# A third key group of the first memory taken from the opening of a two-block transformer kernel and put into the last norm of its first part

## The chip, the cores and the metric

The kernel runs on one core of a Trainium2 chip. The metric is the device time of one execution in microseconds (us); a lower time is better. Three runs of the kernel before gave 1830.6, 1832.58 and 1834.89 us, median 1832.58.

The core has a matrix engine (TensorE, PE in the profile, with PEld for its weight loads), a vector engine (VectorE, DVE), an activation engine (ScalarE, ACT), GpSimd (POOL), and SyncE (SP), which in this kernel only issues DMAs. Each engine works through its own list of instructions in the order in which the list was written, and waits where an operand is not there yet.

## The reference

Two blocks of two layers each work on 256 tokens of 1024 values in float32. What matters here is how the first block begins, how it ends, and what the second block takes from a memory of another 256 tokens (`mem`):

```python
def first_block(x, c, ...):
    c_act = jax.nn.silu(c)
    for l in range(DEPTH):                                     # DEPTH = 2
        mod = c_act @ w_ada[l] + b_ada[l]                      # 6 x 1024 values
        sh1, sc1, g1, sh2, sc2, g2 = [t[:, None, :] for t in jnp.split(mod, N_ADA, axis=-1)]
        h = rmsnorm(x, norm_mix_g[l]) * (1.0 + sc1) + sh1
        z = h @ w_in[l]
        o = jnp.concatenate([swa_mixer(...), mla_mixer(...), nsa_mixer(...), moba_mixer(...)], axis=-1)
        x = x + g1 * (o @ w_out[l])
        h = rmsnorm(x, norm_mlp_g[l]) * (1.0 + sc2) + sh2
        x = x + g2 * (jnp.square(jax.nn.relu(h @ w_up[l])) @ w_down[l])
    return rmsnorm(x, final_norm_g)                            # the "last norm"

def second_block(x, mem, ...):
    for layer in range(DEPTH):
        proj = jnp.einsum('bsd,de->bse', x, w_in[layer])       # z, xbc, dt_raw, ...
        ...
        mem_kv = jnp.einsum('bmd,de->bme', mem, w_mem_kv[layer]).reshape(
            Bsz, MEM_TOKENS, 2, CROSS_HEADS, CROSS_HEAD_DIM)
        oc = _memory_cross_attention(cq, mem_kv)
        ...
```

The keys and values of the memory (`mem_kv`) do not depend on `x`. So the kernel is free to compute those of the second block's first layer, "the first memory", whenever TensorE has nothing else to do.

## The kernel before

**Numbers.** Each float32 matrix is split into a high half and a low half, and each product is made of three matmuls: high by high, low by high, high by low. For a weight, a tile `w` of 128 x 1024 (512 KB, one DMA from SP, L289), the high half `wh` is a cast on ACT (L299) and the low half `wl` a subtraction on DVE (L301). There are 8 buffers for raw weights (`NW`) and 4 for each half (`NS`). `next_w` hands out the next weight and issues loads and splits for those behind it in one long list (`e.wq`, filled by `stream`), so the order of that list is the order of the weights. The weights `w_ada` are used raw by TensorE, and are never split.

**The first memory.** `mem_gemm` makes one of six groups. Groups 0 to 3 are keys (`w_mk` in the profile): two weights, 48 matmuls of 128 x 256 into a bank `g`, and a copy of that bank on ACT into `mk` (L488). Groups 4 and 5 are values (`w_mv`): four weights, 48 matmuls of 128 x 512 into two banks, and two copies into `mv` (L490). Group 4 is called v0 below, group 5 v1, and the key groups k0 to k3.

**The opening.** TensorE runs k0, k1, k2, k3 and v0, and between them the eight pieces `a0` of the first two rows (shift and scale) of `mod`: each piece is two raw weights, 16 small matmuls (`ada`, 128 x 32 by 128 x 256). Which pieces go with which group stands in the table `start`. After four pieces `ada_end` copies the row to `pt1` (ACT, L567), transposes it with matmuls `adat`, and adds the bias on DVE (`mod`, L572). Once the entries tagged `start2` have been issued, the statistics of the first norm are issued: four squares on ACT (L451), which share the two buffers of `pt1` with the row copy; folds on DVE (L438, L444); a matmul `st` that sums over the partitions; `rv` on DVE (L420), `rsy` on POOL (L403), and `bc`, the matmuls that spread the result. `norm_apply` then makes `nt` (DVE, L603), `ah` (ACT, L604) and `al` (DVE, L605), which the first projection's matmuls `g<-ah,wh` and `g<-al,wh` read.

**The last norm of the first block** (L1084 to 1098): `acc`, the accumulators of the last MLP, are added to `x` (L1085); then comes v1, written ahead of `norm_stats(x)`; then the same chain of squares, folds, `st`, `rv`, `rsy`, `bc`; then `x` times `bc` (L1095), split into `xh` (ACT, L464) and `xl` (DVE, L465), which the second block's first matmuls `dt` and `g` read.

**What sets the order.** A scheduler places each instruction by the program's order and by two offsets of priority: splits of weights (`SPLIT_FIRST`, 100) and norms with `ada_end` (`NORM_FIRST`, 200) may move ahead of what was written before them. On DVE the last norm's loop (L1093 to 1097) is kept in its written order.

Of the kernel before, what the change touches and what calls it, by code (L numbers as in the profile page):

```python
# [480 lines left out]
MEM_KEYS = lambda l: [("w2_mk", l, g) for g in range(4)] + [("w2_mv", l, g) for g in range(2)]  # L481


def mem_gemm(e, l, i, hl, mk, mv, tag="mem"):

    key = MEM_KEYS(l)[i]
    if i < 4:
        e.gemm(tag, [key], lambda _: hl, lambda ps: e.nc.scalar.copy(mk[:, 2 * i : 2 * i + 2, :], v3(ps, 2)))  # L488
    else:
        e.tok_gemm(tag, key, hl, lambda ps, t: e.nc.scalar.copy(mv[:, t, (i - 4) * 512 : (i - 3) * 512], ps))  # L490
# [3 lines left out]
def block1(e, ctx, mem0):  # L494
# [3 lines left out]
    mhl, mk0, mv0 = mem0  # L498
# [11 lines left out]
    ad_mlp = lambda l: [(1,0),(1,1)] if l == 0 else [(1,5)]  # L510
    ad_next = lambda l: ada(l+1,2)+ada(l+1,3)
    mlp_keys = lambda l: {1 + 6 * i + n: [("w_ada", *p, n)] for i, p in enumerate(ad_mlp(l)) for n in range(4)}
    MEM = 5
    a0 = ada(0, 0) + ada(0, 1)
    start = [[], a0[0:2], a0[2:4], a0[4:6], []]
    for k in range(MEM):
        e.stream(MEM_KEYS(0)[k], *start[k])
    half = e.wq[-2:]
    del e.wq[-2:]
    e.stream(*a0[6:8])  # L520
# [1 line left out]
    for l in range(DEPTH):  # L522
# [9 lines left out]
                e.stream(("w_down", l, g - 1))  # L532
            e.stream(*nxt.get(g, []))
        e.stream(("w_down", l, 15), *([("w_in1", l + 1, zorder[0])] if l + 1 < DEPTH else []), *ad_next(l))
    e.stream(*MEM_KEYS(0)[MEM:])


    th = e.t(cp, [P, KC], "cth")
# [53 lines left out]
    def ada_add(tag, keys):  # L592
        for key in keys:
            e.add(tag, lambda key=key: (ada_pool if tag == "mlp" else ada_step)(*key[1:]))
# [10 lines left out]
                nc.vector.scalar_tensor_tensor(al[:, k, :], tt, sh[:, k : k + 1], ah[:, k, :].bitcast(F32), ALU.add, ALU.subtract)  # L605


    for g in range(MEM):
        mem_gemm(e, 0, g, mhl, mk0, mv0, f"start{g}")
        ada_add(f"start{g}", start[g])  # L610
    half = e.q[-2:]
    del e.q[-2:]
    ada_add("start4", a0[6:8])
# [470 lines left out]
        for k in range(KC):  # L1084
            nc.vector.scalar_tensor_tensor(x[:, k, :], acc[k // 2][:, (k % 2) * S : (k % 2 + 1) * S], mod[:, 40 + k : 41 + k], x[:, k, :], ALU.mult, ALU.add)  # L1085

    for k in range(MEM, 6):
        mem_gemm(e, 0, k, box[0], mk0, mv0)
    bc = norm_stats(x)
    e.need("mem")  # L1090
# [607 lines left out]
def emit(tc, d, out):  # L1698
    with ExitStack() as ctx:
        e = Emit(tc, d, ctx)  # L1700
        mhl = load_mem(e)
        mk, mv = v3(e.unit("mk"), KC), v3(e.unit("mv"), 2)
        with ExitStack() as inner:
            xh, xl = block1(e, inner, (mhl, mk, mv))
        with ExitStack() as inner:
            block2(e, inner, xh, xl, mk, mv, out)
# [21 lines left out]
```

## Time and profile before

| | before |
|---|---|
| median of 3 runs | 1832.58 us (1830.6 to 1834.89) |
| the profiled execution | 1832.16 us |
| its span (first to last instruction) | 1830.3 us |
| mean granted TensorE clock | 0.991 |
| PE / DVE / ACT busy | 1789.1 / 1333.6 / 1016.8 us |

The profiled execution lies 0.42 us below the median, and its span 1.9 us below its own time. Of the two stretches that the change touches, the opening reaches from 0 to about 62 us, and the last norm from about 744 to 764 us. PE counts as busy as long as its matmuls run, also where they run at the lower of TensorE's two clocks; "PEclk" is the granted share, 1.00 for 2.4 GHz and 0.50 for 1.2 GHz.

### The profile page before, as it was taken

How to read it: one execution, taken by the hardware profiler on the slowest of the kernel's cores; microseconds unless marked ns; L12 is line 12 of the kernel's file. 1: busy time of each engine (PE TensorE's matmuls, PEld its weight loads, DVE VectorE, ACT ScalarE, POOL GpSimd, SP SyncE). 2: the span in 40 equal slices, each digit the busy share in tenths (PEclk: the TensorE clock that was granted, in tenths of full speed). 3: DMA queues.
4: the chain of work that ended last, by engine and by line, in shares of the span. 5: the costliest groups of instructions: out<-in, count | busy, mean ns of one | idle time of the engine just before them, and what ended most of it. 6: DMA issues, size and time to landing. Idle time of an engine off the chain costs nothing.

```text
span 1830.3 us, 36255 instructions
## 1 busy us (share of the span) xinstructions
PE 1789.1 (98%) x14344; PEld 1674.3 (91%) x14344; DVE 1333.6 (73%) x2209; ACT 1016.8 (56%) x1882; POOL 359.1 (20%) x291
## 2 busy tenths in 40 slices
PE   7999999999998999999999999999999999999998
PEld 6778799987888999998999999999999999999997
DVE  4575775756778655798897997576788797997566
ACT  4444444434555444567777575454556777675552
POOL 0000281800007200002444202200001444202200
PEclk9999999999998999999999999999999999999999
DMA  9873876758348655553444644465554445544451
GB/s 335 308 249 138 310 259 199 256 197 306 115 140 299 226 183 185 165 175 121 162 162 151 202 155 144 168 208 173 194 176 133 148 160 162 184 164 165 154 181 67
DMA packets 98219, 346.82 MB, mean 189 GB/s; under 512 B 12288, under 2 KB 13440, under 8 KB 97792
## 3 DMA queue, kind: packets, MB, share of 16 engines
q1 hardware_dynamic: 98048, 344.50, 55.5%
q8 instruction: 112, 1.84, 0.4%
q14 instruction: 59, 0.48, 0.1%
HBM read 339.01 MB, written 1.05 MB: 186 GB/s over the span
## 4 chain that ended last, share of the span: by engine, by line
PE 89%; DVE 4%; DMA 3%; ACT 3%; issue 1%; SPq 0%; POOLq 0%; DVEq 0%; POOL 0%; ACTq 0%
PE g L337 67%; PE acc L337 10%; PE yps L337 2%; DVE wl L301 1%; ACT wh L299 1%; PE ada L337 1%; PE o L337 1%; PE ds L337 1%; PE sc L337 1%; DMA w<-w_in 1%; PE do L337 1%; DMA w<-w_ada 1%; ACT sb L683 1%; PE xo L337 1%; DMA w<-w_up 1%
## 5 line engine op out<-in xcount | busy, mean ns | idle before, releaser
L301 DVE TENSOR_TENSOR wl<-w,wh 128x1024 fp32r<-128x1024 f32 x518 | 660.8, 1279 | 342.8 <-ACT wh L299 341.1
L299 ACT CAST wh<-w 128x1024 fp32r<-128x1024 f32 x518 | 540.5, 1047 | 494.9 <-PE g L337 328.8
L337 PE MATMUL g<-xh,wh 128*128 128x256 f32 x1664 | 478.2, 288 | 0.3
L337 PE MATMUL g<-xl,wh 128*128 128x256 f32 x1664 | 472.6, 284 | 0.0
L337 PE MATMUL g<-xh,wl 128*128 128x256 f32 x1664 | 471.8, 284 | 0.0
L337 PEld LDWEIGHTS g<-xh,wh 128*128 128x128 f32 x1664 | 319.8, 192 | 12.6 <-issue 6.2
L337 PEld LDWEIGHTS g<-xl,wh 128*128 128x128 f32 x1664 | 319.8, 192 | 0.9 <-issue 0.7
L337 PEld LDWEIGHTS g<-xh,wl 128*128 128x128 f32 x1664 | 319.9, 192 | 0.0
L337 PE MATMUL g<-ah,wh 128*128 128x256 f32 x736 | 211.5, 289 | 5.9 <-ACT ah L604 5.4
L337 PE MATMUL g<-ah,wl 128*128 128x256 f32 x736 | 210.6, 287 | 0.5 <-DVE wl L301 0.5
L337 PE MATMUL g<-al,wh 128*128 128x256 f32 x736 | 210.5, 287 | 0.5 <-DVE al L605 0.5
L403 POOL TENSOR_TENSOR rsy<-rv,mhalf 128x2 f32<-128x2 f32 (+1 forms) x14 | 14.5, 1038 | 936.8 <-DVE rv L420 830.1
L337 PE MATMUL acc<-pt,wh 128*128 128x256 f32 x1024 | 182.9, 280 | 0.0
L1505 POOL PARTITION_BROADCAST E<-rows x64 | 98.0, 1592 | 386.7 <-PE tw L1209 190.9
L1504 ACT ACTIVATE E<-E,ltok 128x128 f32<-128x128 f32 x384 | 124.3, 394 | 60.2 <-POOL E L1505 56.8
L337 PEld LDWEIGHTS acc<-pt,wh 128*128 128x128 f32 x1024 | 156.8, 188 | 0.5 <-issue 0.4
L337 PEld LDWEIGHTS g<-ah,wh 128*128 128x128 f32 x736 | 142.7, 195 | 9.8 <-ACT ah L604 6.4
L337 PEld LDWEIGHTS g<-al,wh 128*128 128x128 f32 x736 | 142.8, 194 | 2.7 <-DVE al L605 1.4
L337 PEld LDWEIGHTS g<-ah,wl 128*128 128x128 f32 x736 | 142.8, 194 | 1.2 <-DVE wl L301 0.7
L337 PE MATMUL acc<-pt,wl 128*128 128x256 f32 x512 | 142.3, 279 | 0.0
L583 POOL TENSOR_SCALAR sb<-w,ca 128x1024 f32<-128x1024 f32 x24 | 90.0, 3751 | 59.9 <-PE ada L337 32.8
L337 PEld LDWEIGHTS acc<-pt,wl 128*128 128x128 f32 x512 | 96.2, 188 | 0.0
(384 smaller groups left out, 3404.8 us busy)
## 6 DMA issues: line engine op xcount, KB each, us to landing
w<-w_ada SPq DMA_DIRECT2D x96, 512.0 KB
w<-w_up SPq DMA_DIRECT2D x64, 512.0 KB
w<-w_down SPq DMA_DIRECT2D x64, 512.0 KB
w<-w_br SPq DMA_DIRECT2D x64, 512.0 KB
w<-w_gl SPq DMA_DIRECT2D x48, 512.0 KB
w<-w_in SPq DMA_DIRECT2D x36, 512.0 KB
w<-w_xs SPq DMA_DIRECT2D x32, 512.0 KB
w<-w_z SPq DMA_DIRECT2D x32, 512.0 KB
```

Of the source, the lines that this page charges most:

```text
L299: nc.scalar.copy(wh, w)
L301: nc.vector.tensor_tensor(wl, w, wh.bitcast(F32), ALU.subtract)
L337: self.last_mm = self.nc.tensor.matmul(o, l, r, start=start, stop=stop)
L403: self.nc.gpsimd.tensor_tensor(y, v, self.mhalf[:, 0:cols], ALU.pow)
L583: nc.gpsimd.tensor_scalar(dst, w, ca[:, 2 * n + i : 2 * n + i + 1], None, ALU.mult)
L683: nc.scalar.activation(self.src(i), self.src(i), AF.Exp, bias=nmx[:, i : i + 1], scale=scale, accum_out=den[:, i : i + 1])
L1504: ex = lambda o, s, r: nc.scalar.activation(o, o, AF.Exp, bias=bias[:, s, r : r + 1])
L1505: nc.gpsimd.partition_broadcast(E, state["rows"][32 * (h % 4) : 32 * (h % 4) + 1, :])
```

## The change

The six groups are divided into `early` (k0, k1, k2, v0), which stay in the opening, and `late` (k3, v1), which are made in the last norm, k3 first. The pieces of `a0` that stood behind k3 now stand with those behind k2, so four pieces follow k2 in a row. The tag `start2`, which is waited for ahead of `x`'s statistics, now covers all four of them.

```diff
-    MEM = 5
+    early, late = (0, 1, 2, 4), (3, 5)
     a0 = ada(0, 0) + ada(0, 1)
-    start = [[], a0[0:2], a0[2:4], a0[4:6], []]
-    for k in range(MEM):
-        e.stream(MEM_KEYS(0)[k], *start[k])
+    start = [[], a0[0:2], a0[2:6], []]
+    for i, k in enumerate(early):
+        e.stream(MEM_KEYS(0)[k], *start[i])
     half = e.wq[-2:]
     del e.wq[-2:]
     e.stream(*a0[6:8])
...
-    e.stream(*MEM_KEYS(0)[MEM:])
+    e.stream(*(MEM_KEYS(0)[k] for k in late))
...
-    for g in range(MEM):
-        mem_gemm(e, 0, g, mhl, mk0, mv0, f"start{g}")
-        ada_add(f"start{g}", start[g])
+    for i, k in enumerate(early):
+        mem_gemm(e, 0, k, mhl, mk0, mv0, f"start{i}")
+        ada_add(f"start{i}", start[i])
...
-    for k in range(MEM, 6):
+    for k in late:
         mem_gemm(e, 0, k, box[0], mk0, mv0)
     bc = norm_stats(x)
```

The number of instructions on each engine stays the same; only their order changes.

On TensorE in the opening, before, right behind the two `ada` pieces that follow k2 (`ada_265`) comes k3 (`g_411`), with `adat` inside it, then two more pieces (`ada_469`), `st`, and v0 (`g_500`, `g_507`):

```order
152 L337 MATMUL ada_265<-w_208,ca_11_101 32x256 x4
153 L337 MATMUL g_411<-mh_77,wh_236 128x256
...
176 L337 MATMUL adat_382<-pack_1_70,pt_64_380 128x4 x2
...
203 L337 MATMUL ada_469<-w_276,ca_11_101 32x256 x3
...
206 L337 MATMUL ada_469<-w_295,ca_11_101 32x256 x4
207 L337 MATMUL st_401<-ones_72,fold_392 128x1 x2
208 L337 MATMUL g_500<-wh_323,mh_77 128x512
209 L337 MATMUL g_507<-wh_323,mh_77 128x512
210 L337 MATMUL g_500<-wl_325,mh_77 128x512
```

After, at the same place (`ada_259` is the first row of `mod`, `ada_374` the second, `g_438` and `g_445` are v0):

```order
152 L337 MATMUL ada_259<-w_208,ca_11_101 32x256 x4
153 L337 MATMUL ada_374<-w_264,ca_11_101 32x256 x4
154 L337 MATMUL ada_374<-w_270,ca_11_101 32x256 x4
155 L337 MATMUL adat_370<-pack_1_70,pt_58_368 128x4 x2
156 L337 MATMUL ada_374<-w_276,ca_11_101 32x256 x4
157 L337 MATMUL ada_374<-w_283,ca_11_101 32x256 x4
158 L337 MATMUL g_438<-wh_287,mh_77 128x512
159 L337 MATMUL g_445<-wh_287,mh_77 128x512
160 L337 MATMUL st_426<-ones_72,fold_417 128x1 x2
161 L337 MATMUL g_438<-wl_289,mh_77 128x512
```

The 48 matmuls of k3 are gone from between the row's pieces, and `st` now stands behind the first two matmuls of v0.

On ACT at the same place, after: the copy of k2's bank, the row copy, the four squares, and only then the casts for v0 (`wh_287`, `wh_293`):

```order
12 L488 COPY mk_85<-g_282 128x512
13 L567 COPY pt_58_368<-ada_259 128x256
14 L451 ACTIVATE pt_72_413<-x_411 128x512
15 L451 ACTIVATE pt_73_415<-x_411 128x512
16 L451 ACTIVATE pt_75_419<-x_411 128x512
17 L451 ACTIVATE pt_76_422<-x_411 128x512
18 L299 CAST wh_287<-w_285 128x1024
19 L299 CAST wh_293<-w_291 128x1024
```

Before, two casts for k3 stood between the bank's copy and the row copy, and the copy of k3's bank between the squares and v0's casts.

On DVE in the last norm, before, the four subtractions for the second block's first weights (`wl_8488` to `wl_8506`) all stand ahead of the first two `x` (L1095):

```order
781 L444 TENSOR_TENSOR fold_8355<-fold_8355 128x256
782 L301 TENSOR_TENSOR wl_8500<-w_8496,wh_8498 128x1024
783 L420 TENSOR_SCALAR rv_8367<-st_8364 128x2
784 L301 TENSOR_TENSOR wl_8506<-w_8502,wh_8504 128x1024
785 L1095 SCALAR_TENSOR_TENSOR x_386<-x_386,pack_1_70,bc_8371 128x256 x2
786 L465 TENSOR_TENSOR xl_8431<-x_386,xh_8430 128x256
```

After, at the same place:

```order
778 L444 TENSOR_TENSOR fold_8297<-fold_8297 128x256
779 L301 TENSOR_TENSOR wl_8488<-w_8484,wh_8486 128x1024
780 L301 TENSOR_TENSOR wl_8494<-w_8490,wh_8492 128x1024
781 L420 TENSOR_SCALAR rv_8309<-st_8306 128x2
782 L301 TENSOR_TENSOR wl_8500<-w_8496,wh_8498 128x1024
783 L1095 SCALAR_TENSOR_TENSOR x_411<-x_411,pack_1_70,bc_8313 128x256 x2
784 L301 TENSOR_TENSOR wl_8506<-w_8502,wh_8504 128x1024
785 L465 TENSOR_TENSOR xl_8431<-x_411,xh_8430 128x256
```

The last of the four subtractions now stands between the first two `x` and the first `xl`. On TensorE k3's bank `g_8316` stands between `acc` and v1, and `st` 12 matmuls of v1's last weight and 3 more ahead of `bc`.

## Rows read from the trace of the kernel before

**Rows 1.** The page: busy time of the engines, and the chain of waits by engine
```profile
PE 1789.1 (98%) x14344; PEld 1674.3 (91%) x14344; DVE 1333.6 (73%) x2209; ACT 1016.8 (56%) x1882; POOL 359.1 (20%) x291
...
PE 89%; DVE 4%; DMA 3%; ACT 3%; issue 1%; SPq 0%; POOLq 0%; DVEq 0%; POOL 0%; ACTq 0%
```

**Rows 2.** Windows: length, busy PE, PEld, DVE, ACT, POOL; PEclk, DMA share, GB/s
```profile
40.00:45.00 5.00, 5.00 (x57) 3.93 (x56) 2.84 (x5) 3.52 (x5) 0.00 (x0) 1.00 0.79 296
...
58.00:64.00 6.00, 3.97 (x22) 2.93 (x22) 4.76 (x9) 3.64 (x7) 0.00 (x0) 1.00 1.00 379
...
214.00:221.00 7.00, 6.05 (x26) 5.75 (x27) 6.44 (x15) 3.38 (x8) 3.04 (x2) 0.51 1.02 413
...
528.00:534.00 6.00, 4.55 (x33) 3.63 (x34) 4.85 (x14) 4.34 (x11) 0.00 (x0) 1.00 0.11 33
...
756.00:764.00 8.00, 6.88 (x34) 6.69 (x35) 6.79 (x17) 3.24 (x9) 0.00 (x0) 0.57 0.37 116
764.00:768.00 4.00, 4.00 (x36) 4.00 (x35) 0.03 (x1) 1.10 (x2) 0.00 (x0) 1.00 0.00 0
```

**Rows 3.** The chain of waits: start, length, what
```profile
26.82 5.96 PE g L337 x48
...
743.99 10.47 PE g L337 x46
```

**Rows 4.** PE's timeline, opening: start, length, what [idle before, what ended it]
```profile
32.70 1.93 PE L337 MATMUL ada<-w,ca 128*32 128x256 f32 x32
...
45.47 0.50 PE L337 MATMUL g<-wl,mh 128*128 128x512 f32 x1
...
53.36 0.72 PE L337 MATMUL g<-wh,mh 128*128 128x512 f32 x2
...
61.16 0.38 PE L337 MATMUL g<-ah,wh 128*128 128x256 f32 x1 [1.54 <-ACT ah L604]
```

**Rows 5.** SP's timeline, opening: DMA issues
```profile
25.58 0.80 SPq L289 DMA_DIRECT2D w<-w_mk  x2
26.45 7.75 SPq L289 DMA_DIRECT2D w<-w_ada  x4
```

**Rows 6.** ACT's timeline, opening
```profile
38.86 0.63 ACT L451 ACTIVATE pt<-x 128x512 f32<-128x512 f32 x1 [2.78 <-PE adat L337]
40.25 1.15 ACT L451 ACTIVATE pt<-x 128x512 f32<-128x512 f32 x2 [0.76 <-DVE fold L438]
```

**Rows 7.** DVE's timeline, opening
```profile
42.44 0.43 DVE L444 TENSOR_TENSOR fold<-fold 128x256 f32<-128x256 f32 x1
44.19 1.23 DVE L301 TENSOR_TENSOR wl<-w,wh 128x1024 fp32r<-128x1024 f32 x1 [1.33 <-ACT wh L299]
```

**Rows 8.** PE's timeline, other places where PE waited
```profile
214.43 0.79 PE L337 MATMUL g<-ah,wh 128*128 128x256 f32 x2 [2.31 <-ACT ah L604]
...
529.42 1.44 PE L708 MATMUL tp<-pack,sb 128*128 128x128 f32 x6 [1.80 <-DVE sb L695]
```

**Rows 9.** PE's timeline, last norm
```profile
755.84 0.71 PE L337 MATMUL bc<-pack,rsy 128*128 128x128 f32 x4 [1.05 <-POOL rsy L403]
757.67 0.58 PE L337 MATMUL dt<-xh,wh 128*128 128x256 f32 x1 [1.12 <-ACT xh L464]
...
758.48 0.41 PE L337 MATMUL dt<-xl,wh 128*128 128x256 f32 x1
758.69 0.41 PE L337 MATMUL dt<-xh,wl 128*128 128x256 f32 x1
```

**Rows 10.** DVE's timeline, last norm
```profile
755.56 1.23 DVE L301 TENSOR_TENSOR wl<-w,wh 128x1024 fp32r<-128x1024 f32 x1 [0.58 <-ACT wh L299]
756.71 0.87 DVE L1095 SCALAR_TENSOR_TENSOR x<-x,pack,bc 128x256 f32<-128x256 f32 x2
757.65 0.42 DVE L465 TENSOR_TENSOR xl<-x,xh 128x256 fp32r<-128x256 f32 x1
```

## The prediction, made before the changed kernel had run

> **What bounds the kernel now.** I read the page's busy times first, then its chain: PE is busy for 1789.1 us of the 1830.3 us span and holds 89% of the chain [rows 1]. So what counts is how many matmuls PE has to run, at which clock, and how long it waits. The change leaves the number of matmuls as it is. It can only move time between the two stretches that it touches, so I read the windows of these two next, then the timelines of PE, ACT and DVE in them. The windows show that around the opening's end the DMA engines are at their limit (share 1.00 at 58 to 64 us), but that PE is busy while k3 runs, for 5.00 of 5.00 us at 40 to 45 us, and at full clock [rows 2]. The last norm runs at a low clock, 0.57 from 756 to 764 us, and is back at 1.00 from 764 us [rows 2].
>
> **What goes from the opening.** A key group is 48 matmuls in 5.96 us, 0.124 us each [rows 3]. If nothing replaced it, the opening would be 5.96 us shorter. But k3 was also what PE worked on while the statistics of `x` were made. The two `ada` pieces behind k2 begin at 32.70 and take 1.93 us [rows 4]; up to 34.6 us nothing changes. Now the next two pieces (1.86 us) and `adat` (0.34 us) follow at once, so PE reaches v0 at 34.6 + 2.2 = 36.8 us. Their weights are there: in the list of loads they take the places of k3's two and of the first two behind these, issued at 25.58 us and from 26.45 us on [rows 5], when buffers came free that the change leaves alone.
>
> What isn't there is the first half of v0. Its cast stands behind the four squares on ACT. The second square waits for `adat`, since row copy and squares share two buffers; it began at 38.86 us before [rows 6]. Now `adat` stands behind two of the four weights, at 34.6 + 0.93 = 35.5 us, so the second square can begin at 36.1 us, 2.76 us earlier. From that square on nothing shortens the chain: squares three and four begin 1.39 us later (40.25 - 38.86) and take 1.15 us together [rows 6], so ACT is free at 36.1 + 1.39 + 1.15 - 0.1 = 38.55 us, the first cast takes 1.05 us, and the first v0 matmuls can run at 39.65 us. The folds end at 42.44 + 0.43 = 42.87 us before [rows 7], so at 40.1 us now, and behind them DVE makes the first subtraction, 1.23 us [rows 7]: 41.35 us. PE's third v0 matmul, the first that reads it, begins at 41.4 us, against 45.47 us before [rows 4]. That is 4.1 us. From there on PE's list is as before up to the end of the row's pieces, but for the `st` that has moved ahead (0.3 us): v0's second half, begun at 53.36 us before [rows 4], begins at 48.95 us. I take 4.4 us. So 1.5 to 2 us of the key group's time turn into waiting, 36.8 to 39.65 and, after two matmuls and `st`, 40.3 to 41.4 us: 3.9 us in all.
>
> The first norm's end stays tied to that: `adat` of the second row now stands behind all 24 matmuls of v0's second half, not behind 12 of them, but a subtraction that stood between `A` and `nt` is gone. These two are within 0.5 us of each other, so I cost them at nothing together.
>
> **The clock there.** PE has waits with and without a drop of the clock behind them. A wait of 2.31 us at 214 us is followed by 7 us at 0.51, but one of 1.80 us at 529 us and one of 1.54 us at 61 us are not followed by any [rows 2, 4, 8]. The new wait of 2.85 us, with 1.1 us more close behind, is longer than the longest of these three, so I expect a drop. What a drop costs is read in the last norm: from 758.48 us the 128 x 256 matmuls follow each other at 0.21 us [rows 9], against 0.124 us at full clock, until about 763.8 us. That is 25 matmuls in 5.3 us which would take 3.1 us, so a drop costs 2.2 to 2.3 us. Bounds for this term: 0 (no drop) and 3 us, if the seven microseconds of the spell at 214 us were all spent on matmuls at 0.21 us (33 of them, 0.086 us lost on each). I take 2.3, the row nearest in kind. The opening then gains 4.4 - 2.3 = 2.1 us.
>
> **What comes to the last norm.** Before, v1 holds PE from 743.99 us on for 10.47 us with 46 of its matmuls, 0.2276 us each [rows 3]; two stand earlier, among the last `acc`. Now two matmuls of k3 stand there, 0.2 us shorter, so `acc` ends at 743.8 us. Then come 46 of k3 (46 x 0.12 = 5.5 us; its halves are split ahead, beside `acc`), 48 of v1 (10.9 us) and `st` (0.35 us): `bc` could begin at 760.5 us. It began at 755.84 us, after a wait of 1.05 us for `rsy` [rows 9]. That wait goes, because `st` now stands 15 matmuls (3.4 us) ahead of the end, and `rv` and `rsy` lie beside these. So `bc` comes 4.7 us later: 5.75 us for a key group, less 1.05 us.
>
> Behind `bc` a new link stands on DVE: `bc` to `x` 0.8 us, two `x` 0.87 us, then the subtraction that had been done before the first `x` begins (755.56 us, 1.23 us) [rows 10], then the first `xl`, 0.42 us. The subtraction waits for a cast, which waits for v1's last matmul because it takes that weight's buffer; the cast ends 1.05 us behind it, at 761.5 us, beside `bc` and `x`, and is not the limit. The first `xl` matmul comes 0.8 + 0.87 + 1.15 + 0.42 = 3.2 us behind `bc`'s start, where before it came 758.48 - 755.84 = 2.64 us behind it [rows 9]. On PE `dt` and two `g` wait for `xh` in between, as before. So the second block's matmuls begin 4.7 + 0.6 = 5.2 us later (rounded down, since the 0.2 us at `acc` may be more).
>
> The clock there: before, PE waited 1.05 and 1.12 us around `bc` and the clock fell [rows 2, 9]. Now only the waits behind `bc` are left, 1.3 and 0.5 us. If it falls all the same, the shift is 5.2 us; if not, 5.2 - 2.3 = 2.9 us. I hold the first for likelier (0.6), since the idle time from the last v1 matmul to the first `xl` matmul is much the same.
>
> **The rest.** The order moves by a few rows in the mixers of both layers and ahead of the second block; loads run ahead of PE there, so I take 0, with 1 us on either side.
>
> **The sum.** -4.4 + 2.3 + 5.2 = +3.1 us against the profiled execution's 1832.16 us: 1835.2 us. The median of the runs shown is 0.4 us higher, which is inside the rounding.
>
> **The rivals.**
> (a) Both stretches gain: PE's waits in the opening are too short to lower the clock, and the shorter waits in the last norm leave it high. Then 1832.2 - 4.4 + 2.9 = 1830.7 us; with the key group's whole 5.96 us, if v0's cast were done in the squares' waits, 1829.1 us. For it speaks that the DMA engines are full in the opening and nearly idle after 764 us (share 0.00) [rows 2]; against it that no wait of PE there ends with a DMA, and that ACT's list has the cast behind the squares. The Trainium skill (Perfetto Trace Analysis, Optimization Strategy) says that a kernel whose most-contended engine changes over time may gain when such stretches are interleaved; moving loads from a full stretch into an idle one is that, and by this rule the change would win. The rows show PE, not the DMA, holding both stretches, so I give it little.
> (b) The opening's gain is lost altogether: the clock drops a second time in the first norm's gap, 59 to 62 us, where it stayed at 1.00 before [rows 2] although PE waited 1.54 us and more. It decides if the drop from the v0 wait has not ended when that gap comes. The price is one more drop, 2.3 us: +5.4 us, 1837.5 us, slower.
> (c) One for one: 5.96 us go and 5.75 us come, every wait stays as long as it was: 1832 us. Against it speaks that ACT's and DVE's lists differ around both places.
> (d) The opening loses a drop and the last norm keeps the full clock: -2.1 + 2.9 = +0.8 us, 1833 us.
>
> **How the numbers follow.** Two runs of this kernel can be told apart from about 0.2%, 3.7 us; below 1828.5 to 1829 us is faster, above 1836.3 us slower. Chances: my forecast 0.45 (own range 1833 to 1837.5), (b) 0.15, (d) 0.2, (c) 0.08, (a) 0.12. The forecast lies 1.1 us below the bound for slower and its terms are good to some 1.5 us, so a third of it counts as slower, and nearly all of (b): 0.15 + 0.13 + some of the rest = 0.31. Faster takes the better half of (a), since its best lies at the bound, and some chance for what I do not see: 0.11. The same is left 0.58. The range is 1829.8 to 1838.3 us: from (a) without its best case to (b) with 1 us on top.
>
> **What would show it.** In the opening: PE's timeline with a wait of nearly 3 us ahead of the first `g<-wh,mh` 128 x 512, ended by the cast, and a second of 1.1 us ended by the subtraction `wl`; the third v0 matmul at 41.4 us; PEclk near 0.5 from about 40 to 46 us; the first `al` matmul at 60.3 us, not 62.4 us. In the last norm: `bc` at 760.5 us less the opening's gain, without a wait for `rsy`; on DVE an L301 between L1095 and the first L465; the first `xl` matmul 3.2 us behind `bc`; the clock near 0.55 for 5 us. I am wrong if PE works through to v0 without that wait, or if the second block's first matmuls come less than 2 us or more than 5 us later than before, measured from the span's start.

## The result: slower by half a per cent, outside the predicted range

| | before | after |
|---|---|---|
| median, 5 runs each in the same comparison | 1833.3 us (1830.6 to 1837.27) | 1844.96 us (1839.75 to 1847.94) |
| the profiled execution, its span | 1832.16, 1830.3 us | 1845.25, 1843.5 us |
| its mean granted clock | 0.991 | 0.988 |

The ratio is 1.0052, 95% interval 1.0041 to 1.0064: slower by 9.5 us (0.0052 x 1833.3), 7.5 to 11.7 us. The forecast was 1835.2 us, at most 1838.3. Timed a second time (`after_again` below) the ratio was 1.0052 again.

The page of the kernel after, the lines that answer to [rows 1]:

```profile
PE 1796.3 (97%) x14344; PEld 1680.6 (91%) x14344; DVE 1335.5 (72%) x2209; ACT 1016.7 (55%) x1882; POOL 359.1 (19%) x291
...
PE 90%; DVE 4%; ACT 3%; DMA 2%; issue 1%; POOL 0%; SPq 0%; POOLq 0%; DVEq 0%; ACTq 0%
```

The same 14344 matmuls keep PE busy for 7.2 us more. Up to PE's last matmul the granted clock is low for 41.0 us of this execution, and for 27.3 us of that of before; at half speed the difference costs some 6.9 us (an estimate). So about half of the 13.2 us between the two spans is clock, spread over the kernel; the rest is waits (39.8 against 33.9 us in all).

Windows of the kernel after, columns as in [rows 2]:

```profile
40.00:45.00 5.00, 4.54 (x14) 3.61 (x15) 2.93 (x5) 1.21 (x2) 1.62 (x1) 0.59 1.02 414
45.00:50.00 5.00, 5.00 (x25) 3.24 (x24) 2.11 (x2) 2.71 (x3) 0.00 (x0) 0.73 0.91 353
58.00:64.00 6.00, 3.87 (x19) 3.39 (x18) 5.24 (x13) 3.83 (x8) 0.00 (x0) 0.78 0.99 368
...
771.00:779.00 8.00, 7.66 (x64) 7.46 (x63) 5.44 (x16) 3.49 (x7) 0.00 (x0) 1.00 0.24 76
850.00:858.00 8.00, 6.43 (x48) 5.90 (x47) 7.39 (x13) 6.07 (x9) 4.46 (x5) 1.00 0.71 226
```

The granted clock (the third number from the right) drops at 40 us, as predicted, and again in the first norm at 58 to 64 us, where [rows 2] has 1.00. Behind the last norm it stays high in this execution.

PE's timeline in the opening of the kernel after:

```profile
33.20 2.80 PE L337 MATMUL ada<-w,ca 128*32 128x256 f32 x48
35.92 0.61 PE L337 MATMUL adat<-pack,pt 128*128 128x4 f32 x4
36.46 1.07 PE L337 MATMUL ada<-w,ca 128*32 128x256 f32 x16
40.22 0.73 PE L337 MATMUL g<-wh,mh 128*128 128x512 f32 x2 [2.69 <-ACT wh L299]
...
41.81 0.80 PE L337 MATMUL g<-wl,mh 128*128 128x512 f32 x1 [0.25 <-DVE wl L301]
...
57.97 0.50 PE L337 MATMUL adat<-pack,pt 128*128 128x4 f32 x4
59.99 0.39 PE L337 MATMUL g<-ah,wh 128*128 128x256 f32 x1 [1.52 <-ACT ah L604]
60.86 0.39 PE L337 MATMUL g<-ah,wh 128*128 128x256 f32 x1 [0.48 <-ACT mv L490]
61.37 0.58 PE L337 MATMUL g<-al,wh 128*128 128x256 f32 x1
```

ACT's timeline there, and DVE's:

```profile
36.63 0.63 ACT L451 ACTIVATE pt<-x 128x512 f32<-128x512 f32 x1 [0.53 <-PE adat L337]
38.02 1.15 ACT L451 ACTIVATE pt<-x 128x512 f32<-128x512 f32 x2 [0.76 <-DVE fold L438]
39.12 1.04 ACT L299 CAST wh<-w 128x1024 fp32r<-128x1024 f32 x1
```

```profile
40.54 1.22 DVE L301 TENSOR_TENSOR wl<-w,wh 128x1024 fp32r<-128x1024 f32 x1
```

This is the forecast's chain: PE waits 2.69 us for v0's cast, which stands behind four squares, and `g<-wl,mh` starts at 41.81 us (41.4 foretold). The 128 x 512 matmuls behind it start 0.43 us apart (42.41, 42.84 and 43.26 us), where they start 0.23 us apart once the clock is back at 1.00 (49.01 and 49.24 us). The wait at the first norm, 1.52 + 0.48 us, is as long as before. PE's timeline of the kernel before has, behind the 1.54 us of [rows 4]:

```profile
62.03 0.39 PE L337 MATMUL g<-ah,wh 128*128 128x256 f32 x1 [0.48 <-ACT mv L490]
62.40 0.39 PE L337 MATMUL g<-al,wh 128*128 128x256 f32 x1
```

But after the change the wait ends at a low clock: the first `al` matmul lasts 0.58 us, 0.39 before.

PE's timeline in the last norm of the kernel after, with the wait in the second block that follows, and DVE's:

```profile
768.59 0.61 PE L337 MATMUL bc<-pack,rsy 128*128 128x128 f32 x4
770.68 0.39 PE L337 MATMUL dt<-xh,wh 128*128 128x256 f32 x1 [1.48 <-ACT xh L464]
771.63 0.39 PE L337 MATMUL dt<-xl,wh 128*128 128x256 f32 x1 [0.34 <-DVE xl L465]
...
853.16 0.39 PE L337 MATMUL g<-xh,wh 128*128 128x256 f32 x1 [1.57 <-ACT dv L1311]
```

```profile
769.24 0.87 DVE L1095 SCALAR_TENSOR_TENSOR x<-x,pack,bc 128x256 f32<-128x256 f32 x2 [0.89 <-PE bc L337]
770.03 1.22 DVE L301 TENSOR_TENSOR wl<-w,wh 128x1024 fp32r<-128x1024 f32 x1
771.16 0.42 DVE L465 TENSOR_TENSOR xl<-x,xh 128x256 fp32r<-128x256 f32 x1
```

`bc` has no wait for `rsy` left, and the subtraction stands between `x` and `xl`: against [rows 9, 10] the first `xl` matmul is 771.63 - 768.59 = 3.04 us behind `bc` (3.2 foretold, 2.64 before).

Stage by stage, from traces. One profile is not enough, since one kernel drops its clock at some waits in one execution and not in the next, so these are means over all profiles here with the same order in that stage: four each in the first three rows (of before: `before`, `before_again`, `end_only`, `hold_before`; of after: `after`, `after_again`, `hold_after`, `open_only`), three each in the last two (`before`, `before_again`, `open_only`; `after`, `after_again`, `end_only`).

| stage | before | after | difference | forecast |
|---|---|---|---|---|
| start to first `al` matmul | 62.2 | 60.65 | -1.6 | -2.1 |
| to the first `acc` of layer 0 | 166.65 | 169.45 | +2.8 | 0 |
| to the last `acc` of layer 1 | 517.4 | 518.5 | +1.1 | 0 |
| to the first `xl` matmul | 14.5 | 20.1 | +5.5 | +5.2 |
| to PE's last matmul | 1064.1 | 1064.7 | +0.6 | 0 |
| sum | | | +8.4 | +3.1 |

Of the 5.3 us that the forecast missed, 2.8 lie behind the first norm, in a stage whose work the change leaves as it was, but for the places of some rows. The profiles of one kind spread there: 165.0 to 167.3 us before, 168.3 to 172.0 after, and the longest has one drop more than the others, at 194 us. The 1.1 us of the third row rest on the first profile of before alone (514.1 us, the other three 518.4 to 518.9): the other profiles show no difference there.

### The profile page after: what moved, and what is told of

Same layout as the page of the kernel before. It is cut to its first block, busy times and chain, and to the rows that moved or that the text cites. A ratio compares the mean times of both kernels' runs of the same rounds, so it can differ in the third digit from the quotient of the medians.

```text
span 1843.5 us, 36254 instructions
## 1 busy us (share of the span) xinstructions
PE 1796.3 (97%) x14344; PEld 1680.6 (91%) x14344; DVE 1335.5 (72%) x2209; ACT 1016.7 (55%) x1882; POOL 359.1 (19%) x291
## 3 DMA queue, kind: packets, MB, share of 16 engines
HBM read 339.01 MB, written 1.05 MB: 184 GB/s over the span
## 4 chain that ended last, share of the span: by engine, by line
PE 90%; DVE 4%; ACT 3%; DMA 2%; issue 1%; POOL 0%; SPq 0%; POOLq 0%; DVEq 0%; ACTq 0%
PE g L337 67%; PE acc L337 10%; PE yps L337 1%; PE o L337 1%; DVE wl L301 1%; PE ada L337 1%; PE ds L337 1%; PE sc L337 1%; ACT wh L299 1%; PE do L337 1%; DMA w<-w_in 1%; PE xs L337 1%; PE xo L337 1%; ACT sb L683 1%; PE tp L708 1%
## 5 line engine op out<-in xcount | busy, mean ns | idle before, releaser
L299 ACT CAST wh<-w 128x1024 fp32r<-128x1024 f32 x518 | 540.9, 1047 | 508.0 <-PE g L337 338.3
```

What stands on the lines that cost most here:

```text
L299: nc.scalar.copy(wh, w)
```

## Experiments

Each ran beside the kernel before (medians 1833.9 to 1834.9 us). Differences in us are (ratio - 1) x 1834.

### The two kernels again

`after_again` and `before_again` are the two kernels without an edit.

> The changed kernel itself, a second profile. In its first profile it lost 8.9 us between the first al matmul (61.4 us) and the last acc matmul (751.6 us): 6.2 us by more time at the low clock (new spells at 61.3, 194.5, 416.3 and 535.8 us), 1.7 us by longer waits of PE. Theory A (the spells are a matter of the single execution): the longer waits of 1.05 and 0.82 us near 192 us and of 4.45 us near 561 us return, but the spells stand elsewhere, and at least two of the four are gone. Theory B (the moved rows in the mixers make the spells): all four return at the same places, within 1 us. Time by both: 1840 to 1848 us.

> The kernel before itself, a second profile; ratio 1.000. In its first profile the low clock came at 214, 484, 552 and 757 us only. Theory A: some of these are gone or others stand beside them (near 61, 192, 411 or 530 us, where PE waits 0.4 to 1.8 us), and the time at the low clock differs by several us from 34.4. Theory B: the same four spells again, 34 us in all within 2 us.

Measured: after 1841.48 us (6 runs), ratio 1.0052 [1.0036, 1.0069]; before 1834.63 us (12 runs), 1.0006 [0.9997, 1.0015]. The loss repeats. Windows of `before_again`:

```profile
411.00:418.00 7.00, 6.90 (x44) 4.83 (x44) 5.50 (x15) 2.73 (x6) 0.04 (x1) 0.54 1.01 400
531.00:535.00 4.00, 4.00 (x21) 2.84 (x21) 2.35 (x5) 1.18 (x3) 0.00 (x0) 0.58 0.31 91
```

The profile on which the forecast rested has 1.00 in 528 to 534 us [rows 2], and around 410 us too; a window of the kernel before:

```profile
410.00:420.00 10.00, 8.67 (x86) 5.57 (x86) 6.98 (x18) 3.63 (x8) 0.72 (x1) 1.00 1.00 394
```

The same kernel, in another execution, drops its clock at both, and from the first to the last `acc` row of the table it took 4.4 us more. So a low clock at 416 and 536 us in the first profile of after is no effect of the change by itself.

### Each half of the change alone

`open_only` (k3 is not made at all: a quarter of the keys is left out):

```diff
-    early, late = (0, 1, 2, 4), (3, 5)
+    early, late = (0, 1, 2, 4), (5,)
...
+    nc.gpsimd.memset(mk0[:, 6:8, :], 0.0)
```

> The opening's half of the change alone: k3 leaves the opening and is not made in the last norm (its part of mk is filled with zeros by POOL, so the keys of that quarter are left out). The order of the mixers is that of the changed kernel, the last norm that of before. Theory B: +7.8 us against before, as in the changed kernel's first profile up to the last acc, so about 1841 us. Theory A: opening -1.0, waits in the mixers +1.7, and as many low spells as the execution happens to have: -1 to +4 us, about 1834 us. My forecast on record for this half was -2.1 us.

`end_only` (the kernel before, which makes k3 a second time in the last norm):

```diff
-    e.stream(*MEM_KEYS(0)[MEM:])
+    e.stream(MEM_KEYS(0)[3], *MEM_KEYS(0)[MEM:])
...
-    for k in range(MEM, 6):
+    for k in (3, 5):
```

> The last norm's half alone: k3 stays in the opening and is made a second time in the last norm (48 matmuls more than before). Opening and mixers in the order of before. Both theories: +5.3 us up to the first xl matmul, +1.8 us of waits behind it near 840 us, -2.3 us if the clock stays high there as in the changed kernel: +4.8 us, about 1838 us; with the drop of the clock +7 us.

Measured: `open_only` 1838.52 us (12 runs), 1.0030 [1.0017, 1.0042]; `end_only` 1841.09 us (5 runs), 1.0046 [1.0033, 1.0059]. Taking 48 matmuls out of the opening costs 5.5 us (3.1 to 7.7); the first three rows of the table above sum to 2.3. That is the side on which the forecast failed. The end costs 8.4 us (6.1 to 10.8), where its traces show 6.1 and the forecast had 5.2. The two differences add up to 13.9, not to 9.5 us; only their lower ends (9.2 us) leave room for that, and no run explains more of it.

The granted clock of the runs, averaged over all of them, tells the halves apart: 0.9884 in `open_only`, as in the changed kernel (0.9882), and 0.9918 in `end_only`, as in the kernel before beside them (0.9917). With PE busy for 98% of the span, 0.0033 of the clock is worth some 6 us (an estimate, 0.0033 x 1834). So by this estimate the opening's loss is one of clock, and the end's is not.

### The wait ahead of v0: filled

`fill_wait` (20 matmuls of 128 x 256, whose result nobody reads, queued ahead of v0; in the trace 18 of them run ahead of the last piece and two inside it):

```diff
+    def cover():
+        ps = e.bank("cover")
+        mh = mhl[0]
+        for i in range(20):
+            e.mm(ps[:, 0:S], mh[:, i % KC, 0:P], mh[:, (i + 1) % KC, :], i == 0, i == 19)
+    pos = next(i for i, (t, _) in enumerate(e.q) if t == "start3")
+    e.q.insert(pos, ("start2", cover))
```

> The changed kernel with 20 more matmuls of 128 x 256 (of the memory's high half with itself, into a bank that nobody reads) behind the third of the four weights that follow k2, so that PE works for 2.4 us of the 2.7 to 2.9 us that it waits there for v0's cast. Work is added, none removed. Theory C (that wait lowers the clock there and again in the first norm's gap, about 13 us more low time in an execution): the spell at 38 to 41 us is gone, the first al matmul comes near 57.7 us instead of 59.7 to 61.4, the mean clock of the runs rises from 0.988 to 0.990 or more, time 1838 to 1840 us (-3 to -5 against the changed kernel). Theory D (the low time comes from the mixers' other order): mean clock stays at 0.988, and at most 1 us is gained in all: 1842 us or more.

Measured: 1835.39 us (11 runs), 1.0011 [1.0002, 1.0020]. Against the changed kernel, adding work took 7.5 us away. PE's timeline of `fill_wait`:

```profile
41.65 0.50 PE L337 MATMUL g<-wl,mh 128*128 128x512 f32 x1 [0.47 <-DVE wl L301]
...
50.10 0.60 PE L337 MATMUL adat<-pack,pt 128*128 128x4 f32 x4
...
55.78 0.36 PE L337 MATMUL g<-al,wh 128*128 128x256 f32 x1
```

But two things changed here. The wait for the cast and the low clock behind it are gone (0.47 us for the subtraction are left), and the scheduler put `adat` of the second row behind 2 of v0's 24 matmuls, so that the first norm has hardly a wait (one of 0.59 us at 59.60). The two are taken apart below.

### The wait ahead of v0: its causes

`cast_first` (the squares are issued behind v0's first cast):

```diff
-    bc0 = norm_stats(x)
+    with tc.issue_after(e.casts["w2_mv", 0, 0][0].ins):
+        bc0 = norm_stats(x)
```

> The changed kernel with the squares of x's statistics put behind v0's first cast on ACT (and so v0's first subtraction ahead of the folds on DVE); no work is added, and adat stays behind all of v0's second half, as in the changed kernel. PE's wait ahead of v0 should shrink from 2.7 us to about 1 us. Theory C (the wait for v0 and the low clock behind it are what the opening lost): no spell at 38 to 41 us, first al matmul near 56 us, mean clock 0.990 to 0.991, about -6 us against the changed kernel: 1836 to 1837 us. Theory E (the kernel with added matmuls won by having adat earlier, so that the first norm's wait fell from 2.0 to 0.6 us): that wait stays 2.0 us here, a spell of 3.4 to 6.8 us follows it near 55 us, and the time is 1839 us or more.

Measured: 1841.68 us (5 runs), 1.0036 [1.0022, 1.0049]. PE's waits only shrank to 2.15 + 0.53 us. PE's and ACT's timelines say why (L300 is L299 of the other kernels):

```profile
40.07 0.73 PE L339 MATMUL g<-wh,mh 128*128 128x512 f32 x2 [2.15 <-ACT wh L300]
```

```profile
38.98 1.04 ACT L300 CAST wh<-w 128x1024 fp32r<-128x1024 f32 x1 [3.02 <-DMA w<-w_mv]
```

The cast now waits 3.02 us for v0's weight: behind the squares stood the load, ready at almost the same time. The forecast had named ACT's list alone. Since the wait stayed, and the one at the first norm with it (1.54 + 0.49 us), this run does not tell theory C from theory E.

`open_v0first` (two of the pieces go between v0's halves, so that v0 comes sooner):

```diff
-    start = [[], a0[0:2], a0[2:6], []]
+    start = [[], a0[0:2], a0[2:4], []]
...
-    e.stream(*a0[6:8])
+    e.stream(*a0[4:8])
...
-    ada_add("start4", a0[6:8])
+    ada_add("start4", a0[4:8])
```

> The changed kernel with another order in the opening: the two pieces that had moved behind k2 now stand behind the first half of v0 (a0[4:8] between v0's halves), so that v0's weights are loaded and cast before the squares and PE has v0 to work on during x's statistics. The last norm as in the changed kernel. Theory C: no wait near 37 us, no low clock there, first al matmul at 62.2 - 6.3 = 56 us, mean clock as before (0.9915), and in sum -6.3 in the opening, +6.2 in the last norm and behind it, +0 to 1 in the mixers: 1834 us, no change against before. Theory D: the mixers' low time stays: 1838 us or more, clock 0.988 to 0.989.

Measured: 1844.77 us (5 runs), 1.0059 [1.0045, 1.0073]. The first `al` matmul came at 55.97 us, 4.7 us ahead of the changed kernel's mean, and in this execution all of it was lost at once. PE's timeline, and the window behind it:

```profile
82.99 1.22 PE L337 MATMUL bc<-pack,rsy 128*128 128x128 f32 x4 [2.73 <-POOL rsy L403]
```

```profile
82.00:96.00 14.00, 13.01 (x33) 6.88 (x34) 1.54 (x3) 1.16 (x2) 0.94 (x1) 0.51 0.36 146
```

Here an early start came to nothing: the new order brought a new wait, with 14 us at the low clock behind it.

### The place of `adat`

In the changed kernel `adat` of the second row stands behind all 24 matmuls of v0's second half. `adat_early` puts it behind 12, as before, and the edit names nothing else:

```diff
-    e.q.extend(("start5", fn) for _, fn in half)
+    def behind_adat(fn):
+        with tc.issue_after(e.adat.ins):
+            fn()
+    e.q.append(("start5", half[0][1]))
+    e.q.append(("start5", lambda: behind_adat(half[1][1])))
```

> The changed kernel with one order kept as it was before: adat of the second row stands behind 12 of the 24 matmuls of v0's second half, not behind all 24 (the last 12 are queued behind it). Nothing is added or removed. Its 2.7 us wait ahead of v0 stays, and the spell behind it. The wait of 1.52 + 0.48 us at the first norm falls to 1 us or less. Theory C (the wait for v0 and its low clock carry the loss): -1 to -2.5 us against the changed kernel, 1840.5 to 1842 us. Theory E (the late adat and the first norm's wait, with the spell that follows it near 60 us, carry it): -4 to -7 us, 1836 to 1839 us, and no spell near 60 us.

`fill_late` is `fill_wait` with `adat` forced behind all 24, and `before_late` the kernel before with the same edit:

```diff
     def ada_end(l, s, ps):
+        if (l, s) == (0, 1):
+            e.need("start5")
+            last_v0 = e.last_mm
+            with tc.issue_after(last_v0.ins):
+                ada_end_(l, s, ps)
+        else:
+            ada_end_(l, s, ps)
+
+    def ada_end_(l, s, ps):
```

> The changed kernel with the 20 added matmuls in the wait ahead of v0, but with adat of the second row forced behind v0's last matmul, where the changed kernel has it. No spell near 40 us; the wait of about 2.0 us at the first norm stays, near 55 us. Theory C: 1836 to 1839 us, clock 0.990 or more. Theory E: a spell of 3.4 to 6.8 us follows the first norm's wait, and 1839 to 1842 us.

> The kernel before, with one order of the changed kernel: adat of the second row forced behind all 24 matmuls of v0's second half (12 before). k3 stays in the opening. Theory E (the late adat is what the opening loses, whatever stands ahead of it): PE's wait at the first norm grows from 1.54 us to 2.5 to 4 us, a spell at the low clock follows it, and the kernel is 3 to 7 us slower than before, 1837 to 1841 us. Rival (the late adat costs only behind a spell at v0, as in the changed kernel): the wait grows by 1 us at most, no more than 2 us slower, 1834 to 1836 us.

| wait ahead of v0 | `adat` behind 24 | `adat` early |
|---|---|---|
| left | 1.0052 [1.0041, 1.0064] (after) | 1.0016 [1.0008, 1.0025] (`adat_early`, 1836.52 us, 12 runs) |
| filled | 1.0026 [1.0016, 1.0036] (`fill_late`, 1838.89 us, 9 runs) | 1.0011 [1.0002, 1.0020] (`fill_wait`) |
| none (kernel before) | 1.0027 [1.0017, 1.0036] (`before_late`, 1838.89 us, 9 runs) | 1 (before) |

PE's timeline of `adat_early`, and two of its windows:

```profile
39.67 0.74 PE L337 MATMUL g<-wh,mh 128*128 128x512 f32 x2 [2.62 <-ACT wh L299]
...
54.74 0.50 PE L337 MATMUL adat<-pack,pt 128*128 128x4 f32 x4
...
58.75 0.39 PE L337 MATMUL g<-al,wh 128*128 128x256 f32 x1
```

```profile
40.00:45.00 5.00, 4.79 (x15) 3.73 (x14) 2.48 (x4) 0.78 (x1) 1.62 (x1) 0.53 1.02 409
58.00:64.00 6.00, 5.56 (x40) 4.85 (x40) 5.57 (x12) 4.53 (x9) 0.00 (x0) 1.00 1.01 374
```

The wait and the low clock at 40 us are still there, but at the first norm no wait of 0.3 us or more is left and the clock stays at 1.00: 40 matmuls from 58 to 64 us, not 19. By the runs that is worth 6.6 us of the 9.5 (4.0 to 9.2, both intervals taken together), as theory E had it, and their mean granted clock is 0.9905, not 0.9882.

The place of `adat` is not all that differs, though. The kernel before has `adat` behind 12 as well, and waits 1.54 + 0.48 us. ACT's timeline of `adat_early`, and of the kernel before:

```profile
57.67 0.51 ACT L605 ACTIVATE ah<-nt,mod 128x256 fp32r<-128x256 f32 x1 [1.68 <-DVE nt L604]
58.19 1.05 ACT L299 CAST wh<-w 128x1024 fp32r<-128x1024 f32 x1
```

```profile
59.65 1.04 ACT L299 CAST wh<-w 128x1024 fp32r<-128x1024 f32 x1 [2.02 <-PE g L337]
60.60 0.90 ACT L604 ACTIVATE ah<-nt,mod 128x256 fp32r<-128x256 f32 x2
```

In `adat_early` the scheduler put the first `ah` ahead of a cast that in the kernel before waits for PE's v0 matmuls and holds `ah` up; on DVE a subtraction went back between `A` and `nt`. No run separates these rows from `adat`, so the 6.6 us are the worth of the edit with what moved along. PE's timeline and a window of `fill_late`:

```profile
54.79 0.50 PE L337 MATMUL adat<-pack,pt 128*128 128x4 f32 x4
58.27 0.51 PE L337 MATMUL g<-ah,wh 128*128 128x256 f32 x2 [2.98 <-ACT ah L613]
```

```profile
60.00:65.00 5.00, 5.00 (x34) 5.00 (x33) 4.22 (x10) 2.59 (x7) 0.00 (x0) 0.73 1.03 401
```

Here the first wait is filled and the second remains, with its drop. Filling alone is worth 4.8 us (2.0 to 7.6), so the first wait has a price too; the two gains overlap (both together 7.5 us, not 11.4). With the wait filled, the late `adat` costs only the other 2.8 us (0.3 to 5.2). And PE's timeline of `before_late`:

```profile
59.52 0.50 PE L337 MATMUL adat<-pack,pt 128*128 128x4 f32 x4
63.01 0.50 PE L337 MATMUL g<-ah,wh 128*128 128x256 f32 x2 [2.99 <-ACT ah L613]
```

A late `adat` costs 5.0 us (3.1 to 6.6) even without any wait at v0, though the first `al` matmul comes only 1.1 us later than before (63.53 against 62.40 us). So the rival, that it costs only in company, falls. (In both forced kernels a subtraction stands between `A` and `nt` on DVE, which the changed kernel has behind `nt`, and the wait is about 3 us, not 2.0; so they rather overstate the price.)

### The end: v1 held back

`hold_after`, `hold_before`, `cast_hold`, `fill_hold` and `early_hold` are the changed kernel, the kernel before, `cast_first`, `fill_wait` and `adat_early` with the last quarter of v1 issued behind `bc`, as cover for the waits behind it:

```diff
     bc = norm_stats(x)
-    e.need("mem")
+    spread = e.last_mm
+    e.fill(len(e.q) - 1)
+    with tc.issue_after(spread.ins):
+        e.need("mem")
```

> The changed kernel with the last quarter of v1 (12 matmuls of 128 x 512, 2.7 us) held back behind bc in the last norm. Takes away the waits of 1.48 and 0.34 us behind bc and brings back a wait of some 0.7 us for rsy ahead of it. If the new subtraction between x and xl sets the end (my forecast's price of 0.6 us), the first xl matmul comes 1.1 to 1.8 us earlier. If the waits near 835 and 850 us (1.4 to 2.0 us) grow by what is gained ahead of them, nothing is left: -0 to -1.5 us against the changed kernel, 1841.5 to 1843 us.

> The kernel before with the last quarter of v1 held back behind bc. Takes away the wait of 1.12 us for xh; the wait of 1.05 us for rsy stays. If the low clock behind the last norm (5.2 and 3.4 us of it in the two profiles of before) is worth its 1.5 to 2.3 us: -2.6 to -3.4 us. If the waits near 830 and 845 us come in its place, as in every kernel whose clock stayed high there (1.65 to 1.83 us): -1.1 to -1.7 us, about 1832 us.

> The squares behind v0's first cast, and the last quarter of v1 held back. Theory C: 1836.5 - 1.9 to -4.5 = 1832 to 1834.6 us, no change against the kernel before. Theory E: 1835 us or more.

> The 20 added matmuls in the opening's wait, and the last quarter of v1 held back behind bc in the last norm. If the two are independent: 1835.5 - 4.5 (what holding back gave the changed kernel by the runs; 1.9 us up to the first xl matmul by the profiles) = 1831 to 1833.6 us, as fast as the kernel before or up to 3 us faster.

> adat of the second row behind 12 of 24, and the last quarter of v1 held back behind bc; no added work. If the two are independent: what adat_early gives, less 1.9 us (by the profiles, up to the first xl matmul) to 4.5 us (by the runs of the kernel with v1's quarter held back alone). Theory C: 1836 to 1840 us. Theory E: 1832 to 1837 us.

| kernel | median (runs) | ratio | without the hold |
|---|---|---|---|
| `hold_after` | 1838.59 us (7) | 1.0026 [1.0015, 1.0037] | 1.0052 |
| `hold_before` | 1836.99 us (11) | 1.0016 [1.0008, 1.0025] | 1 |
| `cast_hold` | 1838.38 us (9) | 1.0023 [1.0014, 1.0033] | 1.0036 |
| `fill_hold` | 1831.98 us (12) | 0.9985 [0.9976, 0.9994] | 1.0011 |
| `early_hold` | 1833.16 us (11) | 1.0000 [0.9990, 1.0010] | 1.0016 |

PE's timeline of `hold_after`, and of `hold_before`:

```profile
762.50 0.71 PE L337 MATMUL bc<-pack,rsy 128*128 128x128 f32 x4 [0.25 <-POOL rsy L403]
...
766.02 0.28 PE L337 MATMUL dt<-xl,wh 128*128 128x256 f32 x1
```

```profile
757.20 1.22 PE L337 MATMUL bc<-pack,rsy 128*128 128x128 f32 x4 [2.50 <-POOL rsy L403]
```

With k3 in the last norm there is work enough for both sides of `bc`: the waits there fall from 1.8 to 0.25 us. The gain is 4.8 us by the runs, where 1.5 at most had been expected, and 1.9 us in the trace up to the first `xl` matmul. Without k3 the quarter that is moved behind `bc` is missing ahead of it, and the wait for `rsy` grows from 1.05 to 2.50 us: `hold_before` is 2.9 us slower, where it had been expected to be 1 to 3 us faster. So the moved group has a use at the end, but only with this second edit. `early_hold`, without any added work, is level with the kernel before; `fill_hold` is faster than it by 2.8 us (1.1 to 4.4).

## Why the prediction was wrong

- **The wait for v0 and its clock: right in kind, and in sum by luck.** Foretold 2.85 us for the cast and 1.1 for the subtraction, with a drop from 40 us at a price of 2.3 us. Found 2.69 and 0.25 us, so 1 us less; but the windows from 40 to 50 us (0.59 and 0.73) hold 6.8 us at the low clock, some 3.4 us at half speed (an estimate), so 1 us more. The two errors cancel: the opening gains 1.6 us up to the first `al` matmul, 2.1 foretold.
- **"I cost them at nothing together": the step that failed, with the clock behind it left at 1.00.** The wait itself was sized rightly: the late `adat` and the subtraction that went do cancel, 1.54 + 0.48 us before, 1.52 + 0.48 after. But the stage behind that wait, put at nothing, lost 2.8 us in the profiles, and the opening's half of the change cost 5.5 us by the runs, where a gain of 2.1 was foretold. What I did not ask is what the wait would be without the late `adat`. In `adat_early` it is gone, and with it a drop of the clock. The price of the late row, with what moved along, is 6.6 us in the changed kernel, 2.8 where the wait ahead of v0 is filled, and 5.0 where it is added to the kernel before.
- **Rival (b) was what happened,** with 0.15. I held 1.00 at 59 to 62 us in one profile for the rule. Over the profiles the drop there came in 4 of 4 with the changed opening, in 2 of 4 with the old one, in 0 of 2 with `adat` early and the wait unfilled. But its 1837.5 us fall short too, and what this drop costs by itself is not shown: in the kernel before the stage behind it took 167.14 and 167.25 us with the drop, 164.96 and 167.25 us without.
- **The last norm: right in sum, by luck in part.** +5.2 foretold, +5.5 found. The forecast took it with a fallen clock and gave 2.9 for a high one. In the first profile the clock stayed high (in `after_again` it fell), and nothing was gained by it: behind the norm the waits that a slow PE had covered came up (853.16: 1.57 us), so that what the clock gave, the rest of the second block took back (+0.6 us to PE's last matmul).
- **The base.** The forecast's one profile had no drop at 416 or 536 us. Between two executions of that kernel the stage with these two differs by 4.4 us. The comparisons' medians of before, 1833.9 to 1834.9 us, lie 1.7 to 2.7 us above that profile's time.
- **Interleaving.** Rival (a), built on the rule that moving work from a crowded stretch to an idle one may gain, fell: the opening lost by giving work away. The Trainium skill (Perfetto Trace Analysis, Optimization Strategy) says that "performance may be improved by interleaving those regimes"; here its next step on gaps, to find what blocks the engine that matters, was the one that held.

Open: from layer 0's first `acc` to layer 1's last, three kernels (`adat_early` 514.4, `early_hold` 515.2, `cast_hold` 515.3 us) take 2 to 5 us less than most (517.3 to 519.5), and so does one of the four profiles with the order of before. They miss one or both drops near 410 and 530 us. Whether the early part of the kernel decides that, or chance, no run here settles; it would account for the rest of the 6.6 us, of which the trace up to layer 0's `acc` shows 3.4 (226.74 against a mean of 230.1), and that of `early_hold`, with the same opening, 4.9.

## What to carry to other kernels

Where PE holds the chain, a group of matmuls that fills a norm's statistics is not a cost that can be taken away: ask what PE will wait for when it goes, and price each wait with the clock behind it. A row moved within PE's list, at the same wait as before, can still be an expensive part of a change; ask what the wait would have been without the move, and what the scheduler moves along with it. And read such drops in several profiles: one shows only where they can come.

## What the runs showed of the hardware

- More work, less time: 20 matmuls that nobody reads, put into a wait of 2.7 us, left the changed kernel 7.5 us faster (4.8 with `adat` kept late).
- One kernel's executions differ by up to 9 us (the changed kernel again: 1839.45 to 1848.39 us), along with the mean granted clock (0.990 and 0.986). The Trainium skill (TensorE: Matmul & The Clock Gate, The HAM clock gate) says of the ramp at a kernel's start that the number of matmuls at the low clock varies from run to run, and that the penalty is under 1% of a typical span. The drops here lie inside the kernel, and they vary too: up to PE's last matmul 27.3 and 34.1 us at the low clock in two profiles of the kernel before. The mean granted clocks, 0.991 and 0.988, put their price at about 1%; this change's whole result is 0.52%.
- A drop can be nearly free. In the kernel before, PE runs slowly behind the last norm [rows 2] and then shows no wait of 0.3 us between 830 and 860 us; in `open_only`, with the same order there and the clock at 1.00, it waits 1.28 us, and both need the same time to PE's last matmul within 0.3 us (1064.5 and 1064.2). PE's timeline of `open_only`:

```profile
843.20 0.38 PE L337 MATMUL g<-xh,wh 128*128 128x256 f32 x1 [1.28 <-ACT dv L1312]
```
